# LayerNorm and RMS statistics as two one-pass products of high and low parts, and the squares of the first norm's second half summed on VectorE

## The chip, the cores and the metric

The kernel runs on one core of a Trainium2 chip. The metric is the time of one execution on the device, in microseconds (us); a kernel's time is the median of several runs. A core has five engines that matter here: TensorE (PE in the profile) multiplies matrices, with its weight loads (PEld) beside the products; VectorE (DVE), ScalarE (ACT) and GpSimd (POOL) work element by element; SyncE (SP) issues transfers. Each engine takes its own queue in order. TensorE writes to PSUM, of which a 128x512 float32 bank is the unit here.

## The reference, cut to what matters

One layer of a decoder, for a prompt of 512 tokens and 32 sample tokens (8 sequences of 4). Both go through the kernel side by side, as 544 columns.

```
mix = W_out( sigmoid(g_a) * P_a(SSD(x)) + sigmoid(g_b) * P_b(mLSTM(x)) )
x = LayerNorm(ALPHA * x + mix)              # first norm
x = LayerNorm(ALPHA * x + ConvFFN(x))       # second norm
...
def _layer_norm(x, g, b):
    mu = mean(x, axis=-1)
    var = mean(square(x - mu), axis=-1)
    return (x - mu) * rsqrt(var + EPS) * g + b
def _rms_norm(x, w):
    return x * rsqrt(mean(square(x), axis=-1) + EPS) * w
```

The SSD branch ends in an RMS norm over 1024 channels, and each LayerNorm is over 1024 channels too. Everything is float32.

## The kernel before, in words

Activations lie with channels on the 128 partitions and the 544 tokens along the free axis, so that 1024 channels are eight tiles of 128x544. The tokens are cut into two halves of 272 columns (`HF`), so that one half's product fits a PSUM bank. A mean over channels is therefore a sum over partitions and tiles, and the kernel takes it with a product: a constant 128x128 matrix (`C("ones")`, or `C("mean")`, filled with 1/1024) is the weight, and the result has the sum in every partition.

The big matrix products are done in split form. `split` (lines 77 to 84) makes from a float32 tile a high part in the type float32r with a ScalarE copy, and a low part with a VectorE subtraction. `gemm` (line 160, its products all on line 153) multiplies high by high, high by low and low by high. Weights come by transfers that SyncE issues, 128x1024 at a time, into three `raw` buffers, and are split as well: in `load_w_` (ScalarE on line 141, VectorE on line 143) for weights used once, in `load_kept` (lines 119 and 120) for weights that are kept for two passes. Both are traced at high priority. The statistics' products are not split: they multiply float32 operands as they are.

The order of each engine's queue is not written out by hand. The program is traced in the order of the source, and a scheduler then lays out the queues with a model of the times of its own. `aside` and `tick` trace pieces of one job between the weight loads of another, and `issue_after` holds instructions behind one that is named.

The stages run like this: input projection, SSD and its convolution, the z gate with the RMS norm, the mLSTM heads, the two branch projections, W_out with the first norm, the up-projection of the FFN (44 tiles), the down-projection with the second norm.

**The RMS statistic** (lines 783 to 806). For each of eight tiles ScalarE squares `xs[j]`, and GpSimd sums the squares into `sq` (line 797). Then one float32 product for each half (line 804) takes the mean into `pq`, and ScalarE makes `rsa` from it.

**A LayerNorm** (class `Norm`, lines 161 to 255) is an object for one half; each norm has two. Eight output tiles reach it one after the other.

- The first six (`tile`, lines 1186 to 1191): VectorE adds the product to the scaled residual, GpSimd adds the tile into `self.sum`.
- Then `centre` (lines 1199 to 1210), which is traced between the parts of the seventh tile's product: a float32 product with the ones (line 1202) gives a provisional mean over the six tiles; VectorE turns it into `self.neg` (line 1204) and adds that to the six tiles (line 1206); ScalarE squares each (line 1208); GpSimd sums the squares (line 1210). The squares have two buffers (`lsq`).
- The last two tiles (`late`, lines 1212 to 1222), here tile six and tile seven: ScalarE squares the tile (line 1214); a float32 product accumulates the tile into `pdel` (line 1217), which becomes the correction of the mean. For tile six GpSimd adds the square (line 1219). For tile seven, two float32 products make the variance `pvar`: one of the summed squares (line 1221) and one of the last square (line 1222).
- `finish` (lines 1224 to 1244): the tiles are corrected (lines 1229, 1236 and 1238), the variance (line 1230) and its inverse root are made, and `emit1` or `emit2` writes the result.

In the first norm, `emit1` makes the split operand `X1` of the up-projection (high part on line 1263, low part on line 1264). Its first half is normalised while W_out runs on the second half of the tokens. The second half is normalised while the up-projection multiplies the first half of the tokens for its first six tiles (lines 1342 to 1347); the product's bank is freed by a ScalarE copy to `fraw` (line 1305).

In the second norm the eighth tile is multiplied for the first half alone, then for the second half alone (lines 1389 to 1398), so that the first half's end is hidden and only the second half's stands behind the last product.

Of the kernel before, what the change touches and what calls it, by code (L numbers as in the profile page):

```python
# [7 lines left out]
F32 = mybir.dt.float32  # L8
F32R = mybir.dt.float32r
BF16 = mybir.dt.bfloat16  # L10
AF = mybir.ActivationFunctionType
ALU = mybir.AluOpType
PSUM = bass.MemoryType.PSUM

T = 544
# [35 lines left out]
def hybrid_step(ctx: ExitStack, tc: tile.TileContext, h):  # L51
    nc = tc.nc
    V, S, G, PE = nc.vector, nc.scalar, nc.gpsimd, nc.tensor

    con = ctx.enter_context(tc.tile_pool(name="con", bufs=1))
# [8 lines left out]
    def yt(shape, name, dt=F32):  # L64
        return kt.tile(shape, dt, tag="y", name=name, bufs=31)
# [7 lines left out]
    def ps(name="ps"):  # L73
        return pms.tile([128, 512], F32, tag="ps", name=name)


    def split(hi, lo, src, scale=None):

        if scale is None:
            S.copy(hi, src)  # L80
            V.tensor_sub(lo, src, hi.bitcast(F32))
        else:
            S.activation(hi, src, AF.Copy, scale=scale)
            V.scalar_tensor_tensor(lo, src, scale, hi.bitcast(F32), ALU.mult, ALU.subtract)
# [117 lines left out]
    for k2 in range(4):  # L202
        raw, wh, wl = w_tiles()
        for k in (2 * k2, 2 * k2 + 1):
            c = slice((k % 2) * 512, (k % 2) * 512 + 512)
# [12 lines left out]
            for w, part in ((wh, 0), (wh, 1), (wl, 0)):  # L218
                for i in range(4):
                    d = slice((k % 2) * 512 + i * 128, (k % 2) * 512 + i * 128 + 128)  # L220
                    for p, (a, b) in zip(psf[i], HF):
                        PE.matmul(  # L222
                            p[:, :272], w[:, d], X[k][part][:, a:b],
                            start=k == 0 and w is wh and part == 0, stop=k == 7 and w is wl,
# [8 lines left out]
    def C(name):  # L233
        a, b = _C[name]
        return cst[:, a:b]
# [5 lines left out]
    V.tensor_copy(selw, C("selm"))  # L241
    selm = con.tile([128, 4], F32R, name="selm")
    V.tensor_scalar(selm, C("selm"), -1.0, None, ALU.mult)
    identb = con.tile([128, 128], BF16, name="identb")
    V.tensor_copy(identb, ident)
    mneg32 = con.tile([128, 16, 32], BF16, name="mneg32")
# [86 lines left out]
    for r in range(2):  # L333
        o = aHL[:, 0:256].rearrange("p (c t) -> p c t", c=4)
        hi, fu = (
            x[:, 0:512].rearrange("p (c r t) -> p c r t", c=4, r=2)[:, :, r] for x in (ah.bitcast(F32), acs)
        )
# [445 lines left out]
    sq = yt([128, T], "sqsum")  # L783
    Y = []
    for j in range(8):
# [13 lines left out]
        split(yh, yl, xs[j], scale=P("nw", j))  # L799
        Y.append((yh, yl))  # L800
    rsa = big.tile([128, T], F32, name="rsa")
    for i, (a, b) in enumerate(HF):
        pq = ps("pq")
        PE.matmul(pq[:, :272], C("mean"), sq[:, a:b], start=True, stop=True)
        S.activation(rsa[:, a:b], pq[:, :272], AF.Ln, bias=epsc[:, 2:3])
    S.activation(rsa, rsa, AF.Exp, scale=-0.5)

# [343 lines left out]
    fp = ffn.enter_context(tc.tile_pool(name="fp", bufs=1))  # L1151
# [1 line left out]
    def ft(shape, name, dt=F32):  # L1153
        return fp.tile(shape, dt, tag="fw", name=name, bufs=12)

    def lt(name, bufs):
        return fp.tile([128, 272], F32, tag=name, name=name, bufs=bufs)

    table = "natural_log_exp_and_others"

    class Norm:
# [37 lines left out]
        def centre(self):  # L1199

            c = ps("pcen")[:, :272]
            PE.matmul(c, C("ones"), self.sum, start=True, stop=True)
            self.neg = self.sum
            V.tensor_scalar(self.neg, c, -1.0 / (128 * self.n), None, ALU.mult)
            for k, r in enumerate(self.first):
                V.tensor_add(r, r, self.neg)
                s = self.sq if k == 0 else lt("lsq", 2)
                S.activation(s, r, AF.Square)
                if k:
                    G.tensor_add(self.sq, self.sq, s)  # L1210

        def late(self, k, i):
            s = lt("lsq", 2)
            S.activation(s, self.r[k], AF.Square)
            if i == self.n:
                self.dl, self.va = ps("pdel")[:, :272], ps("pvar")[:, :272]
            PE.matmul(self.dl, C("mean"), self.r[k], start=i == self.n, stop=i == 7)
            if i < 7:
                G.tensor_add(self.sq, self.sq, s)
            else:  # L1220
                PE.matmul(self.va, C("mean"), self.sq, start=True, stop=False)
                PE.matmul(self.va, C("mean"), s, start=False, stop=True)

        def finish(self, n, hold=None):

            dl, rs = self.neg, lt("lrs", 2)
            S.activation(rs, self.dl, AF.Square)
            for k in range(2):
                V.tensor_sub(self.r[k], self.r[k], self.dl)
            V.tensor_sub(rs, self.va, rs)  # L1230
            S.copy(dl, self.dl)
            S.activation(rs, rs, AF.Ln, bias=epsc[:, 0:1])
            S.activation(rs, rs, AF.Exp, scale=-0.5)
            on_pool = 3 if self.split else 2
            for k in range(8 - on_pool, 8):
                G.tensor_sub(self.r[k], self.r[k], dl)
            for k in range(2, 8 - on_pool):
                V.tensor_sub(self.r[k], self.r[k], self.dl)
            yield 1
            for k in range(8):  # L1240
                if k % n == 0:
                    yield 1
                with tc.issue_after(hold.added.ins) if hold and k > 2 else nullcontext():
                    self.emit(k, self.hf, self.r[k], rs)
# [326 lines left out]
```

## Time and profile before

| what | us |
|---|---|
| median of three runs (lowest, highest) | 1089.66 (1089.62, 1089.86) |
| the profiled execution's own time | 1090.07 |
| its span in the profile | 1088.3 |
| TensorE busy | 1071.6 |
| VectorE busy | 658.8 |
| ScalarE busy | 474.7 |
| GpSimd busy | 258.5 |

The granted TensorE clock was 0.995 of full speed. A product is recorded with its whole pipelined length, so the records overlap, and the distance between two starts is what a product costs the queue. A float32 product leaves two records of TensorE, one of the split type leaves one. In a row of the timeline stand the start, the length, the engine, the line, the operation, output and inputs, the count, and in brackets how long the engine idled before it and who ended that. `pcen`, `pdel`, `pvar` and `pq` are the PSUM tiles of the statistics, `lsum` holds the sums of tiles and of squares, `lsq` a square, `xres` the tiles of the first norm and `r` those of the second.

### The profile page before, as it was taken

Reading aid. Unit: us, or ns where it says so; the run is one execution under the profiler, and the core shown is the slowest. Engines: PE = TensorE matmul, PEld = TensorE weight load, DVE = VectorE, ACT = ScalarE, POOL = GpSimd, SP = SyncE. Lnnn points to the kernel's source line nnn. Section 1 sums busy time; section 2 is a strip of 40 time slices with the busy share of each in tenths; the row PEclk is TensorE's granted clock in tenths of the full one; section 3 lists DMA queues with packets and bytes.
Section 4 is the critical chain, followed back from the end, with each engine's and each line's share of the span. In section 5 each row is a group of like instructions: output and inputs, shape, how many; then the busy total and the mean of one; then the engine's idle time right before and its main releaser. Section 6 shows DMA issues by size and latency. Waiting matters only on the chain.

```text
span 1088.3 us, 22330 instructions
## 1 busy us (share of the span) xinstructions
PE 1071.6 (98%) x9191; PEld 1052.9 (97%) x9191; DVE 658.8 (61%) x1203; ACT 474.7 (44%) x900; POOL 258.5 (24%) x481
## 2 busy tenths in 40 slices
PE   9999999999999999999999999999999999999995
PEld 9999999999999999999999999999999999999995
DVE  4988887866655366655643469566565656522265
ACT  4475224456434355333423335555555555411133
POOL 1643224520111111111200034312121212241152
PEclk9999999999999999999999999999999999999998
DMA  7232224331222252775632343112322223232212
GB/s 254 77 95 68 64 61 140 137 98 59 73 84 59 94 175 73 237 231 185 208 108 78 91 136 121 36 59 81 95 81 95 85 90 91 92 92 88 88 54 82
DMA packets 36261, 114.69 MB, mean 105 GB/s; under 512 B 4604, under 2 KB 4860, under 8 KB 36160
## 3 DMA queue, kind: packets, MB, share of 16 engines
q1 hardware_dynamic: 29232, 93.14, 27.5%
q0 software_dynamic: 5296, 17.10, 4.4%
q10 hardware_dynamic: 1632, 3.03, 0.8%
q8 instruction: 72, 1.18, 0.4%
q14 instruction: 29, 0.24, 0.1%
HBM read 98.62 MB, written 14.64 MB: 104 GB/s over the span
## 4 chain that ended last, share of the span: by engine, by line
PE 93%; DVE 3%; issue 1%; ACT 1%; DMA 1%; POOL 0%; ACTq 0%; DVEq 0%
PE mm L153 81%; PE mm L222 1%; PE ps L222 1%; PE pc L1055 1%; PE pi L1045 1%; PE pss L854 1%; PE ps L153 1%; PE pst L541 1%; PE pn L915 0%; PE pn L917 0%; PE pn L916 0%; PE py L550 0%; DVE wl L143 0%; PE pc L917 0%; PE pc L916 0%
## 5 line engine op out<-in xcount | busy, mean ns | idle before, releaser
L143 DVE TENSOR_TENSOR wl<-wraw,wh 128x1024 fp32r<-128x1024 f32 (+1 forms) x140 | 171.5, 1225 | 183.4 <-PE mm L153 119.6
L141 ACT CAST wh<-wraw 128x1024 fp32r<-128x1024 f32 x140 | 145.4, 1039 | 272.5 <-PE mm L153 229.0
L153 PE MATMUL mm<-xh,wh 128*128 128x272 f32 x960 | 248.5, 290 | 0.6 <-ACT craw L415 0.6
L153 PE MATMUL mm<-xl,wh 128*128 128x272 f32 x960 | 248.1, 290 | 0.0
L153 PEld LDWEIGHTS mm<-xh,wh 128*128 128x128 f32 x960 | 180.3, 188 | 2.2 <-ACT craw L415 0.8
L153 PEld LDWEIGHTS mm<-xl,wh 128*128 128x128 f32 x960 | 180.6, 188 | 1.2 <-issue 0.4
L153 PE MATMUL mm<-x1h,wh 128*128 128x272 f32 x608 | 153.5, 288 | 0.0
L153 PE MATMUL mm<-x1l,wh 128*128 128x272 f32 x608 | 153.4, 288 | 0.0
L153 PE MATMUL mm<-xh,wl 128*128 128x272 f32 x960 | 135.8, 289 | 0.0
L153 PEld LDWEIGHTS mm<-xh,wl 128*128 128x128 f32 x960 | 126.9, 188 | 1.1
L153 PEld LDWEIGHTS mm<-x1l,wh 128*128 128x128 f32 x608 | 114.5, 188 | 0.0
L153 PEld LDWEIGHTS mm<-x1h,wh 128*128 128x128 f32 x608 | 114.4, 188 | 0.0
L1311 POOL COPY fo<-fraw 128x2 f32<-128x2 f32 x44 | 34.7, 789 | 205.6 <-ACT fraw L1309 205.6
L153 PE MATMUL mm<-x1h,wl 128*128 128x272 f32 x608 | 82.4, 288 | 0.0
L1318 DVE SCALAR_TENSOR_TENSOR facc<-fraw,prm,facc 128x560 f32<-128x560 f32 x88 | 71.3, 812 | 15.9 <-ACT facc L1314 12.1
L153 PEld LDWEIGHTS mm<-x1h,wl 128*128 128x128 f32 x608 | 78.6, 188 | 0.0
L1058 DVE SCALAR_TENSOR_TENSOR c<-c,wcb,pc 128x258 f32<-128x258 f32 x64 | 28.6, 478 | 23.0 <-PE pc L1055 23.0
L1061 POOL DMA_DIRECT2D out_o_cs<-c x32 | 17.4, 544 | 101.3 <-DVE c L1058 101.0
L1314 ACT ACTIVATE facc<-fraw,prm 128x560 f32<-128x560 f32 x44 | 37.7, 858 | 3.8
L153 PE MATMUL mm<-x1h,keep 128*128 128x272 f32 x192 | 37.3, 292 | 0.8 <-ACT fraw L1305 0.8
L153 PE MATMUL mm<-mh,keep 128*128 128x272 f32 x192 | 36.8, 289 | 0.0
L153 PE MATMUL mm<-yl,wh 128*128 128x272 f32 x128 | 32.7, 288 | 0.0
(731 smaller groups left out, 2295.8 us busy)
## 6 DMA issues: line engine op xcount, KB each, us to landing
wraw<-in_w SPq DMA_DIRECT2D x63, 512.0 KB, 3.5
wraw<-in_wu SPq DMA_DIRECT2D x44, 512.0 KB, 3.5
c<-in_c SPq DMA_DIRECT2D x32, 258.0 KB, 3.6
out_o_cs<-c POOLq DMA_DIRECT2D x32, 258.0 KB, 3.6
wraw<-in_wd SPq DMA_DIRECT2D x16, 512.0 KB, 3.5
wraw<-in_wa SPq DMA_DIRECT2D x8, 512.0 KB, 3.6
wraw<-in_wb SPq DMA_DIRECT2D x8, 512.0 KB, 3.6
wraw<-in_wo SPq DMA_DIRECT2D x8, 512.0 KB, 3.6
```

Of the source, the lines that this page charges most:

```text
L141: last_split[0] = S.copy(wh[:, :n], raw[:, :n])
L143: last_split[1] = V.tensor_sub(wl[:, :m], raw[:, :m], wh[:, :m].bitcast(F32))
L153: PE.matmul(p[:, :272], w, x[:, a:b], start=first and i == 0, stop=last and i == len(xs) - 1)
L222: PE.matmul(p[:, :272], w[:, d], X[k][part][:, a:b], start=k == 0 and w is wh and part == 0, stop=k == 7 and w is wl,)
L541: PE.matmul(pst[r][gps[i], c * 64 : c * 64 + 64], btok[gps[r], c, gps[i]], xdw[gps[r], c, i ^ j % 2], start=True, stop=True,)
L854: PE.matmul(pss[:, tk], k[d][:, tk], q[d][:, tk], start=d == 0, stop=d == 1)
L1045: PE.matmul(pi[32 * hd : 32 * hd + 32, 0:257], qm[:, hd, d], c0[b, hd][:, d, 0:257], start=False, stop=b == 7 and d == 1,)
L1058: V.scalar_tensor_tensor(c[:, d], c[:, d], wcb[:, hd, 4 + b : 5 + b], pc[:, 0:258], ALU.mult, ALU.add)
L1061: nc.gpsimd.dma_start(out=h["o_cs"][hd, b], in_=c)
L1311: G.tensor_copy(fo[:, j, 0:2], raw[:, 512:514])
L1314: S.activation(acc[:, 0:560], raw[:, 0:560], AF.Identity, bias=P("fb", j), scale=P("fw", 3 * j))
L1318: V.scalar_tensor_tensor(acc[:, 0:560], raw[:, t : t + 560], P("fw", 3 * j + t), acc[:, 0:560], ALU.mult, ALU.add)
```

## The change

The constant matrix with 1/1024 is copied once into a float32r tile, `meanr`. A new function, `mean_of`, splits an operand into high and low part (three buffers of the tag `lpart`) and multiplies both with `meanr`, accumulating in PSUM. It takes the place of the float32 product in four places: in the RMS statistic (written out there, on the whole width, with two tiles of the tag `y`), in `centre` (the scale of `self.neg` follows, since the weight is now 1/1024 and not 1), in `late` for tile six, and for the summed squares. This last product is no longer traced at tile seven but at tile six, as soon as GpSimd has added tile six's square. The products of tile seven and of its square stay in float32.

In `centre`, the sum of the squares goes to VectorE for the second half of the first norm (`self.split` is true for the first norm, `self.hf` is 1 for the second half); the other three stay on GpSimd.

```diff
+    meanr = con.tile([128, 128], F32R, name="meanr")
+    V.tensor_copy(meanr, C("mean"))
...
+    sqh, sql = yt([128, T], "sqh", F32R), yt([128, T], "sql", F32R)
+    split(sqh, sql, sq)
     for i, (a, b) in enumerate(HF):
         pq = ps("pq")
-        PE.matmul(pq[:, :272], C("mean"), sq[:, a:b], start=True, stop=True)
+        for n, part in enumerate((sqh, sql)):
+            PE.matmul(pq[:, :272], meanr, part[:, a:b], start=n == 0, stop=n == 1)
...
-    def lt(name, bufs):
-        return fp.tile([128, 272], F32, tag=name, name=name, bufs=bufs)
+    def lt(name, bufs, dt=F32):
+        return fp.tile([128, 272], dt, tag=name, name=name, bufs=bufs)
+
+    def mean_of(p, x, start, stop):
+
+        hi, lo = lt("lpart", 3, F32R), lt("lpart", 3, F32R)
+        split(hi, lo, x)
+        PE.matmul(p, meanr, hi, start=start, stop=False)
+        PE.matmul(p, meanr, lo, start=False, stop=stop)
...
         def centre(self):
             c = ps("pcen")[:, :272]
-            PE.matmul(c, C("ones"), self.sum, start=True, stop=True)
+            mean_of(c, self.sum, True, True)
             self.neg = self.sum
-            V.tensor_scalar(self.neg, c, -1.0 / (128 * self.n), None, ALU.mult)
+            V.tensor_scalar(self.neg, c, -8.0 / self.n, None, ALU.mult)
...
                 if k:
-                    G.tensor_add(self.sq, self.sq, s)
+                    (V if self.split and self.hf else G).tensor_add(self.sq, self.sq, s)
...
         def late(self, k, i):
...
-            PE.matmul(self.dl, C("mean"), self.r[k], start=i == self.n, stop=i == 7)
             if i < 7:
+                mean_of(self.dl, self.r[k], i == self.n, False)
                 G.tensor_add(self.sq, self.sq, s)
+                if i == 6:
+                    mean_of(self.va, self.sq, True, False)
             else:
-                PE.matmul(self.va, C("mean"), self.sq, start=True, stop=False)
+                PE.matmul(self.dl, C("mean"), self.r[k], start=False, stop=True)
                 PE.matmul(self.va, C("mean"), s, start=False, stop=True)
```

## The prediction, made before the changed kernel was run

> **What bounds the kernel now.** I read the totals of the page, then the chain that ended last from 640 us on, then the timelines of the engines around the two LayerNorms. First the page's span, totals and chain shares:
>
> ```profile
> span 1088.3 us, 22330 instructions
> PE 1071.6 (98%) x9191; PEld 1052.9 (97%) x9191; DVE 658.8 (61%) x1203; ACT 474.7 (44%) x900; POOL 258.5 (24%) x481
> PE 93%; DVE 3%; issue 1%; ACT 1%; DMA 1%; POOL 0%; ACTq 0%; DVEq 0%
> ```
>
> TensorE is busy for 98% of the span and carries 93% of the chain. So time comes off in only three ways: fewer TensorE slots, a TensorE wait gone, or a shorter tail behind the last product. The chain prices the slots and shows one wait; its columns are start, length, what:
>
> ```profile
> 645.86 0.46 PE pcen L1202 x2
> ...
> 675.74 0.03 ACT wh L141
> ...
> 677.52 1.76 POOL lsum L1210
> ...
> 679.34 1.76 POOL lsum L1210
> ...
> 681.13 0.03 ACT lsq L1208
> ...
> 681.47 0.38 ACT fraw L1305
> ...
> 686.25 356.11 PE mm L153 x2846
> ```
>
> A statistics product in plain float32, 128x272, shows as two records and takes 0.46 us of the chain. A one-pass product of the same width takes 356.11 / 2846 = 0.125 us. Between 675.74 and 681.47 the chain leaves TensorE and runs through the adds of squares on GpSimd (line 1210) and the ScalarE queue. The timelines show what that costs:
>
> ```profile
> 675.74 1.05 ACT L141 CAST wh<-wraw 128x1024 fp32r<-128x1024 f32 x1 [4.05 <-DMA wraw<-in_wu]
> ...
> 681.13 0.43 ACT L1208 ACTIVATE lsq<-xres 128x272 f32<-128x272 f32 x1 [1.40 <-POOL lsum L1210]
> 681.89 0.39 PE L153 MATMUL mm<-x1h,keep 128*128 128x272 f32 x1 [0.84 <-ACT fraw L1305]
> 677.52 6.10 POOL L1210 TENSOR_TENSOR lsum<-lsum,lsq 128x272 f32<-128x272 f32 x5 [7.93 <-ACT lsq L1208]
> 683.69 0.78 POOL L1219 TENSOR_TENSOR lsum<-lsum,lsq 128x272 f32<-128x272 f32 x1
> ```
>
> A square of the second half sits on ScalarE for 1.40 us, since its buffer (two of them) is still being added by GpSimd. The copy that frees a PSUM bank stands behind it, and TensorE idles 0.84 us for that bank.
>
> **Part 1: the products.** The groups of the products that the change rewrites, two records for each:
>
> ```profile
> L804 PE MATMUL pq<-sqsum,cst 128*128 128x272 f32 x4 | 1.1, 392 | 0.0
> L1202 PE MATMUL pcen<-lsum,cst 128*128 128x272 f32 x8 | 2.5, 392 | 0.0
> L1217 PE MATMUL pdel<-xres,cst 128*128 128x272 f32 x8 | 2.4, 391 | 0.0
> L1217 PE MATMUL pdel<-r,cst 128*128 128x272 f32 x8 | 2.5, 405 | 0.1
> L1221 PE MATMUL pvar<-lsum,cst 128*128 128x272 f32 x8 | 2.5, 391 | 0.0
> ```
>
> So there are 2 products on line 804, 4 on line 1202, 8 on line 1217, of which the four of tile six change and the four of the last tile stay, and 4 on line 1221: 14 become 28 one-pass products. Thirteen of the 14 lie where TensorE is the bound. The fourteenth is line 1221 of the last half, in the tail:
>
> ```profile
> 1074.30 0.29 PE L153 MATMUL mm<-fh__11842,keep 128*128 128x272 f32 x1
> 1074.42 0.62 PE L1221 MATMUL pvar<-lsum,cst 128*128 128x272 f32 x2
> 1075.12 0.73 PE L1217 MATMUL pdel<-r,cst 128*128 128x272 f32 x2
> 1074.62 0.44 DVE L1195 TENSOR_TENSOR r<-r,mm 128x272 f32<-128x272 f32 x1 [0.96 <-PE mm L153]
> ```
>
> It is issued behind the last big product, and it is done while VectorE adds the last tile up to 1075.06. The next product starts 0.06 us after that add either way. Taking it off the tail therefore gains nothing, and its two replacements, now at tile six, cost 0.25 us where TensorE is full. The sum: 13 x 0.46 = 5.98 us less, 28 x 0.125 = 3.50 us more, **2.48 us gained**.
>
> One price can be read in another way. 0.46 / 0.125 is 3.7, not 4. The Trainium skill (FP8 and Floating Point Precision, TensorE Precision Notes) says that true FP32 takes four passes through the array. With four whole slots of 0.125 us the gain would be 13 x 0.50 - 3.50 = 3.0 us; the row has both in one queue, so I keep 2.48.
>
> **Part 2: the adds moved to VectorE.** Five adds of the first norm's second half leave GpSimd, where the five above took 6.10 us. On VectorE a 128x272 add of two SBUF operands costs what line 1206 costs, 2.19 / 6 to 0.43 us, so some 2.1 us for five:
>
> ```profile
> 674.60 2.19 DVE L1206 TENSOR_TENSOR xres<-xres,lsum 128x272 f32<-128x272 f32 x6
> ...
> 677.42 1.21 DVE L143 TENSOR_TENSOR wl<-wraw,wh 128x1024 fp32r<-128x1024 f32 x1
> ...
> 684.68 0.79 DVE L1229 TENSOR_TENSOR xres<-xres,pdel 128x272 f32<-128x272 f32 x2 [4.22 <-ACT lrs L1227]
> 672.00:690.00 18.00, 17.16 (x130) 16.59 (x129) 12.13 (x27) 8.62 (x21) 8.81 (x9) 1.00 0.46 147
> ```
>
> The last row is a stretch of the windows view (PE, PEld, DVE, ACT, POOL). VectorE is busy 12.13 of 18 us and idles 4.22 us before 684.68, which is the wait for this very chain. The adds fit. Each waits on VectorE for a ScalarE square, and behind it stand the low parts of the coming weights (line 143, 1.21 us) and the add of tile six. Against that, an add can stand behind a 1.21 us low part, but no longer behind four other adds of over a microsecond each. So I take the 1.40 us wait as gone, and with it **0.84 us** on TensorE. What is late next is the same copy behind a square that waits for an add behind a low part: at most 1.21 us. Bounds: 0.84 gained to 0.4 lost (1.21 - 0.84).
>
> One rule speaks against the move. The five adds took 6.10 / 5 = 1.22 us each while VectorE was at work, and the one at 683.69, with VectorE idle, took 0.78. The Trainium skill (Perfetto Trace Analysis, Optimizing Scalar/DVE Operations) says that the two share an SBUF read port, so that moving work between them might not help; the rows agree that they slow each other. By it the stall would stay; that case is rival 1 below.
>
> **Part 3: the splits.** Each product's operand now needs a ScalarE copy and then a VectorE subtraction: four in centring, eight at tile six, and one 128x544 wide for the RMS. No row shows a 128x272 copy to this type. The square above (0.43 us) and the weight cast above (1.05 us for 1024 columns) bound it; I take 0.43, as the width is the same. With a subtraction at 0.43 us, an operand is ready about 0.9 us later. In the packed window, three splits and five adds bring VectorE to 12.13 + 1.3 + 2.1 = 15.5 of 18 us. TensorE takes its queue in order, so 0.9 us costs nothing where a product already stood that far behind its operand:
>
> ```profile
> 1038.91 2.80 POOL L1190 TENSOR_TENSOR lsum<-lsum,r 128x272 f32<-128x272 f32 x2 [14.17 <-DVE r L1186]
> 1042.20 0.62 PE L1202 MATMUL pcen<-lsum,cst 128*128 128x272 f32 x2
> ...
> 1043.78 0.62 PE L1202 MATMUL pcen<-lsum,cst 128*128 128x272 f32 x2
> 1055.68 0.79 DVE L1195 TENSOR_TENSOR r<-r,mm 128x272 f32<-128x272 f32 x2 [0.73 <-PE mm L153]
> 1058.48 0.62 PE L1217 MATMUL pdel<-r,cst 128*128 128x272 f32 x2
> ```
>
> The sums were ready at 1041.71 and the products stood at 1042.20 and 1043.78; tile six was ready at 1056.47 and its product stood at 1058.48. These margins are 0.5 to 2.1 us, and the order is laid out again for the new instructions by the scheduler's own clock, which has stood later than the chip here. The variance product is a new case: it moves from behind the last tile to tile six, so it now waits for the GpSimd sum and its split, and everything on TensorE stands behind it. For the centring of the second half in the first norm, the 4.05 us that ScalarE idled before 675.74 for a weight load is cover: its squares could not run earlier than that cast.
>
> The other edge is the normalised second half, which the up-projection waits for:
>
> ```profile
> 691.90 3.39 DVE L1264 SCALAR_TENSOR_TENSOR x1l<-xres,prm,x1h 128x272 fp32r<-128x272 f32 x8
> 693.25 0.29 PE L153 MATMUL mm<-x1l,keep 128*128 128x272 f32 x1
> ```
>
> Its low parts come from 691.90 to 695.29, TensorE reads the first at 693.25, and it never waits: there is little slack. TensorE will now arrive about 1.5 us earlier (0.84, and the three products of this half at 0.46 - 0.25). The chain gains about 2 to 4 us at the adds (6.10 down to between 2.1 and, with low parts between, some 4) and loses 0.9 at the split of the sum; the two about keep step.
>
> For all new TensorE waits I take **0.6 us**: 0.3 at this edge, 0.3 over the 14 places. The bounds are 0 and two low parts standing ahead of a split, 2.4 us.
>
> At nothing I cost the copy of the constant and the RMS split:
>
> ```profile
> 19.50 0.22 DVE L245 CAST identb<-cst 128x128 bf16<-128x128 f32 x1
> ...
> 24.14 0.96 DVE L143 TENSOR_TENSOR wl<-wraw,wh 128x768 fp32r<-128x768 f32 x1 [4.09 <-ACT wh L141]
> 242.36 1.37 POOL L797 TENSOR_TENSOR sqsum<-sqsum,sq 128x544 f32<-128x544 f32 x1 [4.76 <-ACT sq L796]
> L804 PE MATMUL pq<-sqsum,cst x4: 392/392/393, 246.4 to 247.1; 128*128 128x272 f32 x4
> ```
>
> A cast of that size takes 0.22 us, in front of 4.09 us of idle VectorE. The RMS sum is ready at 243.73 and its product stands at 246.4: 2.7 us for a split of at most twice 0.9. Without this cover TensorE would wait for that split, 1.8 us.
>
> **The sum.** 2.48 + 0.84 - 0.6 = 2.7 us off the profiled span: 1088.3 to 1085.6. The profiled execution took 1090.07 us, so 1.77 lie around its span, and it was 0.41 above the median of 1089.66 (runs 1089.62 to 1089.86). From the median: **1087.0 us**. A measurement of this kernel can tell about 0.2% from no change, which is 2.2 us, so the forecast lies just past that mark.
>
> **Rivals.**
> 1. *The stall stays, or the edge gives back what was won.* The adds wait on VectorE as they did on GpSimd, or the normalised second half does not come earlier. For: the small slack at 693.25, and VectorE at 15.5 of 18 us. Against: a VectorE add is 0.43 us, not 1.2 (6.10 / 5). Price: 0.84 not gained, 0.6 still lost: 2.48 - 0.6 = 1.9 gained, 1087.8; with waits of 1.5, towards their upper bound, 1.0 gained, 1088.7. Chance 0.25.
> 2. *Products stand too early.* The moved variance product reaches TensorE's head before the GpSimd sum is split, at four places, each up to 0.9 us: 3.32 - 3.6 is 0.3 lost, 1089.9. Against: the margins above. Chance 0.08.
> 3. *Slower: VectorE becomes the bound between 672 and 695 us.* Five adds in lockstep with squares hold a place each of 0.86 us (square and add), 4.3 us, and three splits of 0.9 us another 2.7. If all 7.0 stands between the weights' low parts and TensorE, less the 2.48 gained, it is 4.5 slower, 1094.2. It decides once VectorE and its waits take over 18 - 12.13 = 5.9 us in that window. Against: the 4.22 us idle is mostly the wait for these adds. Chance 0.05.
> 4. *The change does not do what it says*: the split products run at the plain price, 28 x 0.46 - 5.98 = 6.9 slower, 1096.6. Against: every big product with this type and width runs at 0.125. Chance 0.02.
>
> **How the numbers follow.** The forecast, 2.2 to 3.5 us gained, has 0.60. Rival 1 is within 0.2% nearly whole, and so is rival 2: 0.33. Rivals 3 and 4 are slower: 0.07. The range runs from all of 3.32 with no new wait, 1086.3, and one wait of a low part's length (1.21 us) less elsewhere in the new order, 1085.1, up through rival 1 and most of the way to rival 2, to 1089.2.
>
> **What would show it.** Right: the groups of lines 804, 1202, 1221 and half of 1217 gone, 28 products of the mean at 0.29 us a record and 0.125 a slot; no TensorE wait on the copy of line 1305; the last tile's product 0.06 us behind its add as before. Wrong: a TensorE wait on a low part of a statistic, on line 1264's tiles or on a weight's low part near 680 to 695 us, or a tail longer than the 13.7 us from 1074.62 to the span's end.

## The result and the profile after

| kernel | median of its runs, us (lowest to highest) | span, us | ratio to before, 95% interval |
|---|---|---|---|
| before | 1089.76 (1089.62 to 1090.23) | 1088.3 | |
| after | 1097.18 (1095.95 to 1097.90) | 1096.1 | 1.0066 [1.0052, 1.0081] |

The changed kernel is slower by 0.66%, some 7.4 us. The forecast was 1087.0, the range ended at 1089.2, and slower had a chance of 0.07. The prediction was wrong in sign.

The totals and the chain shares of the page after:

```profile
span 1096.1 us, 22348 instructions
PE 1072.9 (98%) x9191; PEld 1054.2 (96%) x9191; DVE 664.7 (61%) x1222; ACT 480.3 (44%) x913; POOL 253.1 (23%) x476
PE 91%; DVE 4%; ACT 2%; issue 1%; DMA 1%; POOL 1%; ACTq 0%; DVEq 0%
```

TensorE's share of the chain fell from 93% to 91%; VectorE, ScalarE and GpSimd each have a point more. TensorE is busy for only 1.3 us more than before. So the loss is mostly waiting. The view of TensorE's waits after (us in total, times, the longest) names it:

```profile
PE mm L153 <- DVE x1l L1278: 2.0, 1, 2.0
PE mm L153 <- ACT x1h L1277: 1.9, 1, 1.9
...
PE pdel L1168 <- ACT lpart L80: 1.1, 1, 1.1
PE pw L900 <- DVE vl L81: 0.9, 1, 0.9
...
PE mm L153 <- ACT hmt L822: 0.5, 1, 0.5
...
PE mm L153 <- ACT fraw L1319: 0.4, 1, 0.4
```

Five of these are new: the two of X1 (lines 1277 and 1278, formerly 1263 and 1264), the one on `lpart`, and those on `vl` and `hmt`, 6.4 us together. (A sixth, of 0.5 us on `pdel` in line 1235, is the slot in the tail that the variance product left; the tail is no longer for it.) The old wait on the copy to `fraw` fell from 0.8 to 0.4.

Where the time was lost can be read by matching each product of TensorE with the same one in the trace of before, and subtracting the starts:

| stretch of before, us | after minus before at its end, us | added in it |
|---|---|---|
| 0 to 240, before anything that changed but the constant | 0.35 | 0.35 |
| 240 to 300, RMS norm | 1.95 | +1.60 |
| 640 to 670, W_out, second half of the tokens | 1.32 | -0.63 |
| 670 to 706, second half of X1 | 7.15 | +5.83 |
| 706 to 1040, up- and down-projection | 7.11 | -0.04 |
| 1040 to 1050, second norm, centring | 6.75 | -0.36 |
| 1050 to 1071, second norm, tile six | 7.84 | +1.09 |
| the tail | 7.8 | 0 |

The gain that was forecast is in it: 0.63 is three products at 0.46 less 0.25, and 0.36 is about two. But three places give back 8.5.

**Place 1, X1's second half.** The chain of waits after, from the normalisation on (start, length, what):

```profile
674.56 0.03 DVE lpart L81
674.59 3.49 DMA wraw<-in_wu
...
678.10 1.05 ACT wh L141
...
691.37 0.12 PE pvar L1168
...
694.12 3.39 DVE xres L1275 x8
...
697.98 14.07 PE mm L153 x91
```

and the timeline of the engines after (idle time before, and its ender, in brackets):

```profile
674.48 0.43 DVE L81 TENSOR_TENSOR lpart<-lsum,lpart 128x272 fp32r<-128x272 f32 x1
674.83 2.49 DVE L120 TENSOR_TENSOR keep<-wraw,keep 128x512 fp32r<-128x512 f32 x4
677.24 0.43 DVE L1216 TENSOR_SCALAR lsum<-pcen 128x272 f32<-128x272 f32 x1
...
688.05 0.42 ACT L80 CAST lpart<-lsum 128x272 fp32r<-128x272 f32 x1 [0.48 <-POOL lsum L1231]
688.50 0.44 DVE L81 TENSOR_TENSOR lpart<-lsum,lpart 128x272 fp32r<-128x272 f32 x1 [1.40 <-ACT lpart L80]
691.21 0.28 PE L1168 MATMUL pvar<-lpart,meanr 128*128 128x272 f32 x1
691.71 0.29 PE L1169 MATMUL pvar<-lpart,meanr 128*128 128x272 f32 x1
691.83 0.62 PE L1236 MATMUL pvar<-lsq,cst 128*128 128x272 f32 x2
```

Measure each step from W_out's last product (671.16 before, 672.48 after). The provisional mean is made (line 1216, formerly 1204) 2.5 us behind it before and 4.8 us behind it after: its split's subtraction stands in VectorE's queue among the low parts of kept weights, and the mean itself behind four more. TensorE's queue is late as well: it has the low product at 676.76, 1.9 us behind its low part, so that the mean could not have come before 677.05. VectorE is late to begin with, at the first half: its last low part of X1 ends 1.5 us behind W_out's last product, where before it ended 0.4 us ahead of it. A weight's transfer, which the chain shows behind VectorE (674.59), is late too. The cast of this weight, behind which the squares stand on ScalarE, comes 5.6 us behind W_out (678.10), where before it came 4.6 us behind it (675.74). The sum of squares is complete at 13.3 and at 15.5 us, so the delay is kept through the adds. Then the low part of the sum is ready at 688.94, but TensorE's queue has its product only at 691.71. The last product of the variance starts at 14.5 before and at 19.4 after. From there on the two kernels do the same, and X1's last low part ends at 24.1 and 28.3 us.

**The clock.** During the second of these waits TensorE's clock falls to half. The windows view of after (PE, PEld, DVE, ACT, POOL busy, then granted clock, DMA share, GB/s), and of before in the second fence:

```profile
698.00:702.00 4.00, 4.00 (x18) 4.00 (x18) 2.81 (x7) 0.07 (x1) 0.00 (x0) 0.50 0.02 4
```

```profile
698.00:702.00 4.00, 4.00 (x35) 4.00 (x34) 1.42 (x2) 2.69 (x7) 0.86 (x4) 1.00 0.00 0
```

TensorE is called busy for all of 698 to 702 in both, but the view counts 18 products against 35. The chain has 14.07 us for 91 products, which at the 0.126 us of before would be 11.5: 2.6 us for the clock, by estimate. With the two waits (3.9), less three products (0.63) and the half of the `fraw` wait that went (0.4), that makes 5.5 of the 5.8 us lost here.

**Place 2, the RMS norm.** GpSimd, VectorE, ScalarE and TensorE after, then ScalarE before:

```profile
242.71 1.37 POOL L799 TENSOR_TENSOR sqsum<-sqsum,sq 128x544 f32<-128x544 f32 x1 [4.78 <-ACT sq L798]
...
246.36 0.72 DVE L81 TENSOR_TENSOR sql<-sqsum,sqh 128x544 fp32r<-128x544 f32 x1
...
249.34 0.63 ACT L853 ACTIVATE wt<-wt 128x512 f32<-128x512 f32 x1 [4.56 <-DVE wt L852]
249.99 1.28 ACT L810 ACT_TABLE_LOAD   x1
251.28 0.87 ACT L810 ACTIVATE rsa<-pq,epsc 128x272 f32<-128x272 f32 x2
252.17 1.28 ACT L811 ACT_TABLE_LOAD   x1
...
254.96 0.58 ACT L80 CAST vh<-pv 128x512 fp32r<-128x512 f32 x1
...
249.46 0.50 PE L809 MATMUL pq<-sql,meanr 128*128 128x272 f32 x2
...
256.32 0.50 PE L900 MATMUL pw<-wHL,selw 128*128 128x512 f32 x1 [0.88 <-DVE vl L81]
```

```profile
243.90 1.28 ACT L805 ACT_TABLE_LOAD   x1
247.03 0.94 ACT L805 ACTIVATE rsa<-pq,epsc 128x272 f32<-128x272 f32 x2 [1.85 <-PE pq L804]
247.99 1.28 ACT L806 ACT_TABLE_LOAD   x1
...
250.37 0.57 ACT L80 CAST vh<-pv 128x512 fp32r<-128x512 f32 x1
```

Before, the table of the logarithm was loaded while ScalarE waited. After, the sum is ready at 244.08 and its low part at 247.08, and the low product stands 3 us later (249.46 against 246.4). An exponential of the mLSTM goes first, and both table loads stand between it and the cast to `vh`, for whose low part TensorE waits.

**Place 3, the second norm, tile six.** ScalarE, GpSimd, VectorE and TensorE after:

```profile
1066.29 0.43 ACT L1220 ACTIVATE lsq<-r 128x272 f32<-128x272 f32 x1 [0.41 <-POOL lsum L1222]
1066.63 0.40 ACT L80 CAST lpart<-r 128x272 fp32r<-128x272 f32 x1
...
1056.27 12.73 POOL L1222 TENSOR_TENSOR lsum<-lsum,lsq 128x272 f32<-128x272 f32 x10 [7.44 <-ACT lsq L1220]
...
1062.43 0.79 DVE L1207 TENSOR_TENSOR r<-r,mm 128x272 f32<-128x272 f32 x2 [1.78 <-PE mm L153]
...
1067.09 0.40 PE L1168 MATMUL pdel<-lpart,meanr 128*128 128x272 f32 x1 [1.05 <-ACT lpart L80]
```

Tile six was ready at 1063.22, but the copy for its high part ran at 1066.63. ScalarE takes its queue in order, and squares stood ahead whose two buffers GpSimd was still adding. A product without a split waits for VectorE alone; a split one waits for ScalarE's queue too.

### The profile page after: what moved, and what is told of

It is laid out like the page before. It is cut to its first block, busy times and chain, and to the rows that moved or that the text cites. A ratio compares the mean times of both kernels' runs of the same rounds, so it can differ in the third digit from the quotient of the medians.

```text
span 1096.1 us, 22348 instructions
## 1 busy us (share of the span) xinstructions
PE 1072.9 (98%) x9191; PEld 1054.2 (96%) x9191; DVE 664.7 (61%) x1222; ACT 480.3 (44%) x913; POOL 253.1 (23%) x476
## 4 chain that ended last, share of the span: by engine, by line
PE 91%; DVE 4%; ACT 2%; issue 1%; DMA 1%; POOL 1%; ACTq 0%; DVEq 0%
PE mm L153 78%; PE mm L222 1%; PE ps L222 1%; POOL lsum L1222 1%; PE pc L1060 1%; PE pi L1050 1%; PE ps L153 1%; PE pst L543 1%; PE pss L859 0%; PE pn L920 0%; PE pn L922 0%; PE pn L921 0%; DVE wl L143 0%; PE py L552 0%; PE pc L921 0%
## 5 line engine op out<-in xcount | busy, mean ns | idle before, releaser
L153 PE MATMUL mm<-x1h,keep 128*128 128x272 f32 x192 | 39.7, 299 | 2.3 <-ACT x1h L1277 1.9
L153 PEld LDWEIGHTS mm<-x1h,keep 128*128 128x128 f32 x192 | 32.1, 196 | 3.0 <-ACT x1h L1277 2.1
```

What stands on the lines that cost most here:

```text
L153: PE.matmul(p[:, :272], w, x[:, a:b], start=first and i == 0, stop=last and i == len(xs) - 1)
```

## The experiments

The theory at the outset: the splits lengthen the chains behind them, that of the RMS norm and that of X1's second half. Rivals: the adds on VectorE do it; any edit gives a new order and with it a loss; the loss is the second norm's. Line numbers shift by a few between the kernels.

**The constant alone.** Before, with the lines that make `meanr` and nothing that uses it.

> The kernel before with nothing but the copy of the constant matrix into a float32r tile, which nothing reads. Theory 1 (the splits lengthen two chains: the one to the RMS scale and the one to the second half of the up-projection's operand): no change, 1089.7, and the same TensorE waits as before (0.84 us on the PSUM copy). Rival 2 (the adds on VectorE cause the loss): no change either. Rival 3 (any edit makes the scheduler lay out other queues, and the loss is a bad draw): a shift of 1 us or more, up or down, with waits in other places.

1090.06 against 1090.09, ratio 1.0000 [0.9991, 1.0010]. This edit, as such, costs nothing.

**The RMS split alone.**

```
+    meanr = ...
+    split(sqh, sql, sq)
-        PE.matmul(pq[:, :272], C("mean"), sq[:, a:b], start=True, stop=True)
+        for n, part in enumerate((sqh, sql)):
+            PE.matmul(pq[:, :272], meanr, part[:, a:b], start=n == 0, stop=n == 1)
```

> The kernel before with the RMS statistic alone split. Theory 1: the second product of the RMS mean comes so late that the Ln of the RMS scale falls behind the first mLSTM head's Exp, so that the ScalarE table loads (1.28 us each) stand in front of that head's copies and TensorE waits about 2 us near 255 us; less the 0.4 us of two products, 1091.3, 1.6 slower. Rivals 2 and 3: 0.4 faster or no change, 1089.3 to 1089.7.

1091.54, ratio 1.0015 [1.0006, 1.0025]. The waits on `vl` (0.9) and `hmt` (0.5) are there: place 2 is the RMS split's own.

**The adds alone.**

```
-                    G.tensor_add(self.sq, self.sq, s)
+                    (V if self.split and self.hf else G).tensor_add(self.sq, self.sq, s)
```

> The kernel before with the five adds of squares of the first norm's second half on VectorE and nothing else. Theory 1: the 0.84 us wait goes or is replaced by about as much, 1088.8 to 1089.8. Rival 2: the adds stand behind the weights' low parts, the normalised second half comes 2 to 4 us later, 1091.5 to 1094.

1089.47, ratio 0.9996 [0.9986, 1.0005]: 0.6 us below the constant alone, which is not clear of the noise, but TensorE's wait for the copy to `fraw` is gone from the view of waits. The adds are not the cause; the rival falls.

**After, with the adds back on GpSimd.**

> The changed kernel with those five adds back on GpSimd. Theory 1: still slower than before by 4 us or more, 1094 to 1098, with TensorE waiting for the normalised second half near 690 to 700 us. Rival 2: the waits there are gone and only the RMS loss is left, 1089 to 1091.

1096.07 (1093.89 to 1097.88), ratio 1.0054 [1.0039, 1.0069], with waits of 2.0 on x1l and 1.0 on x1h. The loss stays without the adds.

**The first norm alone, the second norm alone**, each with the adds and without the RMS split. The edit is a condition on each use of `mean_of`:

```
-            mean_of(c, self.sum, True, True)
+            if self.split:          # the other kernel: if not self.split
+                mean_of(c, self.sum, True, True)
+            else:
+                PE.matmul(c, C("ones"), self.sum, start=True, stop=True)
...
```

> Adds on VectorE, and of the split products only those of the first norm (its centring, tile six and the moved variance product); the RMS and the second norm stay in float32. Theory 1 (the splits stand in the chain that ends in the second half of the up-projection's operand): TensorE waits for that half for 2 us or more near 690 us, 1092.5 to 1094.5. Rival 4 (the loss in the norms is the second norm's: its wait for a split operand and a longer tail): 1089 to 1090.

> Adds on VectorE, and of the split products only those of the second norm. Theory 1: one TensorE wait of about 1.2 us on a split operand of tile six and 0.35 us more in the tail, less the 0.8 us of the products: 1090 to 1090.5. Rival 4: 1092 or more.

The first norm: 1095.06, ratio 1.0046 [1.0031, 1.0061], waits of 2.0 and 1.9 on X1. The second: 1089.98, ratio 1.0000 [0.9990, 1.0009], with the wait of 1.1 on `lpart`, which eats its gain. Against the adds alone (1089.47) the first norm's splits lose 5.6 us, the greater part of the loss.

**The variance product alone, the centring alone**, in the first norm, with the adds. In the one only the product of the summed squares is split and moved to tile six; in the other only `centre` is split.

> Adds on VectorE, and of the split products only the moved variance product of the first norm. Theory 1, form a (the split of the summed squares, at the end of the chain, lengthens it most, by 2.7 of the 5 us by the two traces): 1 to 2.5 us of waits near 690 us, 1090.5 to 1092. Form b (the centring's split lengthens it, as it waits on VectorE behind the weights' low parts): 1089.2 to 1089.6.

> Adds on VectorE, and of the split products only the centring of the first norm. Theory 1, form b: 1 to 2.5 us of waits near 690 us, 1090.5 to 1092. Form a: 1089.0 to 1089.5.

The variance product: 1093.13, ratio 1.0023 [1.0013, 1.0033], a wait of 2.0 on x1l. The centring: 1090.21, 1.0002 [0.9993, 1.0011], a wait of 1.0. Against the adds alone that is 3.7 and 0.7 us, and the 0.7 alone would not be clear of the noise. The nine runs of the variance product form two groups, four at 1091.5 to 1092.0, the traced one among them, and five at 1093.1 to 1094.0; the last section comes back to this.

**Is it the split or the move?** The variance product of the first norm was both split and moved. Both kernels here have the adds on VectorE and change no other product. In one kernel it is moved and left in float32; in the other it is split and stays at tile seven.

```
             if i < 7:
                 ...
+                if i == 6 and self.split:      # moved, not split
+                    PE.matmul(self.va, C("mean"), self.sq, start=True, stop=False)
...
             else:
                 ...
-                PE.matmul(self.va, C("mean"), self.sq, start=True, stop=False)
+                mean_of(self.va, self.sq, True, False)      # the other kernel: split, not moved
```

> The adds on VectorE, and in the first norm the product of the summed squares moved to tile six but left in float32, without a split; no other product is changed. Theory (the split costs, its copy and subtraction in the queues of ScalarE and VectorE): no TensorE wait on x1l over 0.5 us, 1089.5, as with the adds alone. Rival (the move costs, since TensorE's queue stands behind a product that needs the GpSimd sum): a wait of 1.5 to 2.0 us on x1l and 1091 to 1093, as with the move and the split together.

> The adds on VectorE, and in the first norm the product of the summed squares split but traced at tile seven, where it stood before; no other product is changed. Theory (the split costs): a wait of 1.5 to 2.0 us on x1l, 1091 to 1093. Rival (the move costs): no such wait, 1089.3.

Moved: 1089.23, ratio 0.9994 [0.9985, 1.0003], no wait on X1. Split: 1093.50, ratio 1.0029 [1.0018, 1.0040], a wait of 2.0 on x1l. It is the split. The timelines of the two, GpSimd's last add of squares, the split and the products, the moved one first:

```profile
682.98 0.78 POOL L1235 TENSOR_TENSOR lsum<-lsum,lsq 128x272 f32<-128x272 f32 x1 [13.36 <-DVE lsum L1223]
...
686.42 0.62 PE L1244 MATMUL pvar<-lsq,cst 128*128 128x272 f32 x2
```

```profile
683.90 0.78 POOL L1235 TENSOR_TENSOR lsum<-lsum,lsq 128x272 f32<-128x272 f32 x1 [14.18 <-DVE lsum L1223]
685.24 0.43 DVE L81 TENSOR_TENSOR lpart<-lsum,lpart 128x272 fp32r<-128x272 f32 x1
...
688.54 0.29 PE L1166 MATMUL pvar<-lpart,meanr 128*128 128x272 f32 x1
688.67 0.62 PE L1244 MATMUL pvar<-lsq,cst 128*128 128x272 f32 x2
```

In float32 the last product starts 2.66 us behind the sum (683.76 to 686.42), split 3.99 us (684.68 to 688.67). The split itself takes 0.99 us of this; the rest is the place in TensorE's queue, 2.87 us behind the low part. So the margin that the product had was not used up by the split: the order laid it out anew on top. The other half of the loss lies earlier: the sum is complete 12.8 us behind W_out's last product when moved, and 14.0 when split; the provisional mean comes 1.2 us later, and the run on the first half, below, shows how that can come about.

**The second norm with its adds on VectorE.** The kernel is the one with the second norm's splits alone, and its first half's adds go to VectorE too.

```
-                    (V if self.split and self.hf else G).tensor_add(self.sq, self.sq, s)
+                    (V if self.split == bool(self.hf) else G).tensor_add(self.sq, self.sq, s)
```

> As the run with the second norm's splits alone, but the adds of squares of the second norm's first half also go to VectorE. Theory (TensorE's 1.1 us wait on a low part comes from a ScalarE queue in which a square waits for a buffer that GpSimd is still adding): the wait on lpart falls below 0.3 us and the time to 1088.7 to 1089.1. Rival (the split's own latency, a copy and a subtraction): the wait stays near 1 us, 1090.0.

1088.81, ratio 0.9990 [0.9981, 0.9998]; the wait on `lpart` is gone. Place 3 is ScalarE's queue behind GpSimd's adds, not the split's own time. What these adds would gain on VectorE without the splits was not run.

**The RMS split, two orders.** One kernel traces it at high priority; the other forces ScalarE's order.

```
+        with tc.issue_after(root.ins):      # root: the exponential that makes rsa
             S.activation(wt, wt, AF.Exp)
```

> The RMS split alone, with its split, products and logarithms traced at high priority. Theory (the 1.4 us lost with the RMS split come from ScalarE's order: the logarithm's table load behind the exponential of line 853, then the casts for TensorE behind both): the wait on vl near 256 us falls below 0.3 us, 1089.7 to 1090.1. Rival (the split's latency of some 2 us in the RMS chain itself): 1091.0 to 1091.6.

> The RMS split alone, with one order forced: the exponential of line 853 on ScalarE is issued behind the one that makes rsa, as in the kernel before. The low products stay where the scheduler laid them, behind the products into pss. Theory A (most of the loss is ScalarE's order, the logarithm's table load of 1.28 us standing behind that exponential): the table load goes back into idle time, TensorE's wait on vl falls below 0.3 us, 1090.0 to 1090.6. Theory B (the loss is the later slot of the low product, 249.4 instead of 246.4 us, and the order only shares it out): the casts for TensorE come at most 0.5 us earlier, the wait on vl stays over 0.5 us, 1091.0 to 1091.6.

High priority: 1091.61, ratio 1.0016 [1.0007, 1.0025]; the order at this place did not change (the exponential at 251.05, the table load behind it at 251.69, the low product at 251.16), so this run tells nothing of the theory. The forced order: 1091.17, ratio 1.0008 [0.9999, 1.0017]. The wait on `vl` is gone, as theory A had it, but waits of 0.4 on `sw` and 0.2 on `hmt` took its place, the logarithm ran at 249.56, not at 247.03, and the time is the one that theory B named. So the order is some 0.4 of the 1.5 us lost, within the spread of the runs. That the greater part is the later low product fits, but no run moved this product back.

**The splits away from the edge.** All of the change but the RMS split and the splits of the first norm's second half, with the second norm's adds on VectorE. The first norm's second half is thus the same as with the adds alone.

> All of the change but the RMS split and the splits in the first norm's second half, and with the second norm's first half also adding its squares on VectorE. Theory (the splits cost only where the chain behind them has no slack): no wait on x1l, x1h, lpart or vl over 0.5 us, and three products more at the lower price than the run with the second norm's splits on VectorE: 1088.81 less 3 x 0.21 is 1088.2. Rival (a split in the first half also reaches the edge, since it shares ScalarE and VectorE with the weights' splits): 1089.0 to 1090.5.

1090.25, ratio 1.0004 [0.9995, 1.0013], with a wait of 1.4 on x1l: the rival was right. VectorE in this kernel, and then with the adds alone:

```profile
671.42 0.90 DVE L1286 SCALAR_TENSOR_TENSOR x1l<-xres,prm,x1h 128x272 fp32r<-128x272 f32 x2
672.25 2.49 DVE L120 TENSOR_TENSOR keep<-wraw,keep 128x512 fp32r<-128x512 f32 x4
674.66 0.43 DVE L1217 TENSOR_SCALAR lsum<-pcen 128x272 f32<-128x272 f32 x1
```

```profile
670.04 2.25 DVE L1264 SCALAR_TENSOR_TENSOR x1l<-xres,prm,x1h 128x272 fp32r<-128x272 f32 x4
672.21 3.09 DVE L120 TENSOR_TENSOR keep<-wraw,keep 128x512 fp32r<-128x512 f32 x5
675.22 0.43 DVE L1204 TENSOR_SCALAR lsum<-pcen 128x272 f32<-128x272 f32 x1
```

W_out's last product starts at 670.85 here and at 672.54 with the adds alone. The first half's last low part ends 1.5 us behind it here (672.33), and 0.25 us ahead of it there (672.29). VectorE then does the weights' low parts without a pause, and the second half's provisional mean comes 3.8 us behind W_out instead of 2.7. Of these 1.1 us some 0.6 is TensorE's own gain, the three products of the first half, which bring W_out's end forward; the rest is delay. So a split in the first half, which TensorE never waits for, reaches X1's second half through VectorE's queue.

**Tile six of the first norm alone**, with the adds; here `pdel` of tile six alone is split, for both halves.

> The adds on VectorE, and of the first norm's splits only the one of tile six into pdel, both halves. Theory (a split costs where its product is the last that the chain waits for; pdel's product of tile six is not, the last square and the variance come later): no new wait, two products at 0.21 us less, 1089.0 to 1089.3. Rival (any ScalarE copy and VectorE subtraction in the second half's window delays X1): a wait of 0.5 to 1.5 us on x1l, 1090 to 1091.

1090.17, ratio 1.0000 [0.9991, 1.0009], a wait of 0.8 on x1l. The theory that this split would be free fell. The provisional mean comes 3.2 us behind W_out, 0.5 later than without it.

**What gained, together**: the adds, the second norm's splits with its adds on VectorE, and in the first norm the move alone.

> What gained in the other runs, together: the adds of squares on VectorE in the first norm's second half and the second norm's first half, all of the second norm's splits, and in the first norm the product of the summed squares at tile six, unsplit. Theory (the edge of X1 is untouched when nothing of the first norm is split, so the gains add): 1088.81 with the second norm alone, less the 0.24 that the move gained beside the adds, is 1088.6, with no new wait over 0.5 us. Rival (a new order gives it back at the edge of X1): a wait of 0.5 to 1.5 us on x1l, 1089.5 to 1090.5.

1088.78 (1088.39 to 1090.81), ratio 0.9988 [0.9979, 0.9997], and no new wait over 0.5 us. It beats both kernels, by 1.2 us against before, and is level with the second norm and its adds alone (1088.81): the 0.24 that was expected from the move is not seen.

## Why the prediction was wrong

**Part 1, the price of the products: right.** A one-pass product of the mean takes 0.12 to 0.13 us of the chain (691.37 above), and where no wait came with it the forecast gain is there to 0.06 us: 0.63 in W_out, 0.36 of 0.42 at the second norm's centring. The one that left the tail changed nothing, as said: from the start of the last big product to the end of the span 14.0 us before (1074.30 to 1088.3) and after (1082.14 to 1096.1).

**Part 2, the adds: right on TensorE, wrong on the chain.** Alone they gained 0.6 of the 0.84 forecast, not clear of the noise, and the wait went. The Trainium skill (Perfetto Trace Analysis, Optimizing Scalar/DVE Operations) says that work moved between GpSimd and VectorE might not help, as they share an SBUF read port. By that the stall would have stayed; the run with the adds alone, where the wait of 0.84 us is gone, does not bear it out here. But the edge was reckoned with 2 to 4 us that the chain would gain at the adds. From the provisional mean to the sum of squares took 10.8 us before (673.65 to 684.47), 10.1 with the adds alone (675.22 to 685.30) and 10.8 after (677.24 to 688.02). The chain there waits for more than GpSimd: squares stand among weight casts on ScalarE, and adds among weights' low parts on VectorE.

**Part 3, the splits: the step that failed.** "0.9 us costs nothing where a product already stood that far behind its operand" took the margin as slack that the split would use up. The runs show two things in its place. First, the margin is made anew: the split variance product stands 2.87 us behind its low part (split at tile seven). Unsplit it stood 0.7 us behind the sum before, 2.1 with the adds alone, 2.2 when moved and 3.0 with the splits away from the edge. So the split's 0.99 us came on top of a margin and did not use it up. Second, the split's two steps stand in the queues of ScalarE and VectorE, and delay what follows in them: the provisional mean comes 0.5 to 2.3 us later behind W_out, even from splits in the other half, and at most 0.6 of this is TensorE's own gain. The text named the first (the order "is laid out again") and still took 0.3 for 14 places.

**The edge at X1: wrong.** "The two about keep step", 0.3 us, became 1.9 and 2.0 us of waits and 2.6 us of half clock. The prediction had read the little slack at 693.25 rightly, but of the chain's two terms one (a gain of 2 to 4 us) was 0 to 0.7, and the other (0.9) was 2.6 after (3.8 us from the sum to the last product of the variance, against 1.2 before). The weight's cast, with 4.05 us of idle ahead of it as cover, was taken as fixed, but it came 1.0 us later itself.

**The RMS split at nothing: wrong.** The cover of 2.7 us was measured to the product's old place, and the split was to take at most 1.8. It took 3.0 us (244.08 to 247.08), as its subtraction stood in VectorE's queue behind a weight's low part (245.21 to 246.44). The product then stood 2.4 us further back, at 249.46, and behind it the logarithm lost its idle place for the table load. 1.5 us lost in the run of its own, which with two products saved (0.4) means about 1.9 us of delay, of which the view of waits names 1.4.

**Tile six of the second norm: not seen.** The margin of 2.0 us at 1058.48 was measured to VectorE's add. A split adds ScalarE's queue to what the product waits for, and there the squares of both halves stood.

**All new waits**: 0.6 forecast with bounds of 0 and 2.4; 6.4 measured, and the clock on top. Rival 3 had the place and the sign, and its 1094.2 is below what came, but its mechanism did not occur: VectorE did not become the bound.

```profile
672.00:690.00 18.00, 17.57 (x138) 17.23 (x137) 14.70 (x33) 9.36 (x21) 0.77 (x1) 1.00 0.46 147
```

In the windows view after, VectorE is busy 14.70 of 18 us there, against 12.13 before (15.5 were forecast): it has room, but what the chain needs stands late in its queue.

**What stays open.** Why the order lays the split products 2 to 3 us behind their operands was not settled; high priority did not move the one that was tried. Of the nine runs with the variance product alone one was traced, at full clock; half clock in the slower five would fit, but was not seen, and before had single runs at 1092 as well.

## What to carry to other kernels

A cheaper instruction that needs two more steps on other engines is priced by the queues that these steps join: ask for each what already stands ahead of it, and what behind it is now late, in the other half too. A gap between an operand and the product that reads it is no slack that a longer operand uses up, if the order is laid out anew. Put such splits where nothing near waits for the chain (here the second norm gained 0.7 us against the adds alone, once its own adds had left GpSimd and ScalarE's queue was freed), and leave them out where a chain already ends just in time.

## What the runs showed of the hardware

TensorE's clock fell to half, in the stretch of X1, in four traces: after, with the adds on GpSimd, with the first norm alone, and with the variance product split at tile seven. No wait there was over 2.0 us. The waits do not settle it: the kernel with the variance product moved and split has the same two waits as the one with it split at tile seven, 0.3 and 2.0 us with four products between them, and its clock stayed in the trace.

The times of the changes settle it, read from the granted clock in slices of 1 us. In each of the four traces the clock falls here and again at the kernel's end, and the two falls lie 389.12 us apart (694.77 and 1083.89 with the split at tile seven, 696.56 and 1085.68 after). The half clock here lasts 3.4 us in three of them and 6.8 us in after. As 389.12 us is 114 times 3.413, a grid of windows of this length fits them all: one and two windows at half clock, and 114 from fall to fall. The moved and split kernel falls only at its end, at 1079.77; counted back by 113 windows, an edge lies at 694.06, within its wait of 2.0 us (692.95 to 694.93). The windows view cut at these edges, for that kernel and then for the one with the split at tile seven, up to its fall:

```profile
690.65:694.06 3.41, 2.04 (x15) 1.61 (x13) 2.99 (x8) 2.84 (x8) 0.00 (x0) 1.00 0.00 0
694.06:697.48 3.42, 2.55 (x20) 2.55 (x21) 3.42 (x9) 1.24 (x4) 0.00 (x0) 1.00 0.00 0
```

```profile
691.36:694.77 3.41, 1.17 (x8) 0.74 (x6) 3.41 (x9) 3.41 (x9) 0.00 (x0) 1.00 0.00 0
```

With 2.04 and 2.55 us of TensorE's work in the two windows the clock stayed; with 1.17 us in one it fell. In the other three traces the window before the fall held 0.94 us (after), 0.88 and 0.76. In after TensorE then worked 1.99 us of the first window at half clock, and a second one followed; in the other three it worked at least 3.15 us, and the clock came back. So the same waits can cost the half clock in one execution and not in another, by where the edges lie. The two groups of runs with the variance product alone, whose means are 1.7 us apart, and those of after, 1095.95 and 1096.53 against 1097.84 and 1097.90, would fit this (3.4 us at half clock lose 1.7), but one run of each kernel was traced.

The Trainium skill (TensorE: Matmul & The Clock Gate, Part 1: The HAM clock gate) says that the clock is halved after an idle window of about 3.4 us, and that such windows run freely. The length agrees with the traces, 3.413 us, and so does the free run, 114 windows from fall to fall; but a window with 1.17 us of work in it was idle enough.
